# Moving the second group's token rows behind the first modulation's weights, and ordering two helpers behind the first features

## Chip, cores and metric

The kernel runs on one core of one Trainium2 chip. The metric is device time in microseconds: the time of one launch, read as the median of several runs. Lower is better.

## What is computed

One step of a hybrid backbone on 128 context tokens and 1024 latent tokens, width 1024, one layer. The part that matters here is the head of the layer:

```python
def rmsnorm(x, w):
    y = xf * lax.rsqrt(jnp.mean(xf * xf, axis=-1, keepdims=True) + EPS)
    return (y * w.astype(F32)).astype(x.dtype)
...
m = jax.nn.silu(cond) @ w_ada_l + b_ada_l          # six shift/scale/gate vectors of 1024
...
h = rmsnorm(x, norm1_w) * (1 + sc1) + sh1
aq, ak, av, mq, mk, mv, mo, mg = jnp.split(h @ w_in, SPLIT_POINTS, axis=-1)
```

Context tokens take their modulation from `c_ctx`, latent tokens from `c`. After this come grouped-query attention, a bidirectional mLSTM, an output projection and a SwiGLU FFN; none of these is edited.

## The kernel before, in words

The 1152 tokens are nine blocks of 128 (`NB`), taken as three groups of three blocks (`CB`). The tiles x3_0, x3_1 and x3_2 (in views of the profile all called x) hold the rows of the groups. For each group, `normalise(c)` squares the rows on ScalarE with a running sum (L355), takes a reciprocal square root on VectorE by twelve small steps (L127 to L133) and scales the rows on VectorE (L358). `turn(c)` transposes the blocks on TensorE (L116) through PSUM banks and copies one half of each block back on ScalarE (L371) and one on VectorE (L372). `features(c)` applies the modulation: on ScalarE it makes the f16 high part of the features (L507), on VectorE the full value (L508) and the difference (L137), which is the low part. `linear_tok` with `kvg_pairs` then multiplies the features by the key, value and gate columns, three products per piece (L483 to L485), the third of which needs the low part; `evac_kvg` takes the result out on ScalarE (L492, L493) and VectorE (L496, tile G).

The modulation that this needs, shift1 and scale1, is the product of the conditioning with two 1024 x 1024 slices of `w_ada`. They arrive as sixteen loads of 512 KB (L295, tiles aw). TensorE multiplies them in four strips (L341), the strips are copied to SBUF on ScalarE and VectorE (L388, tile part) and turned to columns (L347). From the largest shift and scale follows a power of two (tiles hbd, pv, hsc; L171, L161 to L164, L175, L176) by which both are scaled (L402) before the first feature.

The weights of a projection are held as f16 pairs with a power-of-two scale of their own. `Scaled.ready` loads the raw weights (iraw; kraw for the key, value and gate columns; L193), sums absolute values on ScalarE (L198, tile jkw), reduces them on VectorE (L200) and takes the maximum through TensorE (L116, L171, L161 to L164, L175). `groups_in[0]` are the query weights, the next ones those of the mLSTM heads.

All these loads are issued by SyncE, one behind the other. `ada_rest` loads and multiplies the remaining modulations: eight-row pieces a4 (L422), four buffers, released by the strips on TensorE (L341); at the end of a half it stores a row to g_d (L454) and loads the next bias row (L448).

Each engine runs its instructions in a fixed order that the tile scheduler makes from the order of the code. `tc.high_priority(n)` (`hot`) lets a block go ahead of what was written before it. `tc.issue_after(ins)` keeps what a block issues on the engine of `ins` behind `ins`. `weave` interleaves the units of a generator with those of another.

Of the kernel before, what the change touches and what calls it, by code (L numbers as in the profile page):

```python
# [13 lines left out]
AF = mybir.ActivationFunctionType  # L14
# [7 lines left out]
KD = D // P  # L22
NB = 9
# [10 lines left out]
CB = 3  # L34
# [11 lines left out]
def hybrid_step(ctx: ExitStack, tc: tile.TileContext, I: dict, O: dict):  # L46
# [236 lines left out]

    for b in range(2 * CB):
        load_x(b)
# [6 lines left out]
    for n in range(2):  # L292
        for k in range(KD):
            aw = awp.tile([P, D], F32, name=f"aw0_{n}_{k}")
            dma(aw, w_ada[k * P : (k + 1) * P, n * D : (n + 1) * D])  # L295
            ada_w[n].append(aw)
    for b in range(2 * CB, NB):
        load_x(b)
# [74 lines left out]

    for c in range(2):
        normalise(c)
        turn(c)
    emit(kvg_steps)
# [18 lines left out]
    with hot(300):  # L396
        dve.tensor_reduce(out=hs2, in_=shift1, axis=AX.XY, op=ALU.max, apply_absolute_value=True)
        dve.tensor_reduce(out=hbd, in_=scale1, axis=AX.XY, op=ALU.max, apply_absolute_value=True)
        dve.scalar_tensor_tensor(out=hbd, in0=hbd, scalar=float(D) ** 0.5, in1=hs2, op0=ALU.mult, op1=ALU.add)
        emit(power_scale(gp, one1, hbd, hsc[:, 2:4]))  # L400
        for t in (scale1, shift1):
            dve.tensor_scalar(out=t, in0=t, scalar1=hsc[:, 2:3], scalar2=None, op0=ALU.mult)  # L402
        kvg.inverses()
    es_h = ExitStack()
    kvp = es_h.enter_context(tc.tile_pool(name="kvp", bufs=1, side="right", reuse_waits="tile"))
# [92 lines left out]
    def features(c):  # L498
# [3 lines left out]
        for k in range(KD):  # L502
            full = p0.tile([P, CB, P], F32, name=nm("full"), tag="full", bufs=4)
            for i, n in ((0, 1), (1, 2)) if c == 0 else ((0, CB),):
                cnd = 0 if n == 1 else 1
                s, t = scale1[:, k, cnd : cnd + 1], shift1[:, k, cnd : cnd + 1]
                act(hh[:, k, i : i + n], v[:, k, i : i + n], AF.Identity, scale=s, bias=t)  # L507
                dve.tensor_scalar(out=full[:, i : i + n], in0=v[:, k, i : i + n], scalar1=s, scalar2=t, op0=ALU.mult, op1=ALU.add)  # L508
            sub(hl[:, k], full, hh[:, k], "dve")

    for c in range(NCH):
        with hot(100):
            features(c)
        prods = linear_tok(kvg_pairs, 0, 272, evac_kvg, (tuple(range(c * CB, c * CB + CB)),), bank if c == 1 else bankA)
        if c > 0:
            weave(prods, chain(steps, ada), KD, 10)
        else:
            emit(prods)
        if c == 0:
            normalise(2)  # L520
        if c == 1:
            turn(2)
    emit(steps)
# [1065 lines left out]
```

## Time and profile before

| | |
|---|---|
| three runs | 1562.04, 1564.69, 1565.68 us; median 1564.69 |
| the profiled execution | 1563.28 us, of which the span of the trace is 1561.5 |
| busy, share of the span | PE 95%, PEld 80%, DVE 65%, ACT 49%, POOL 17% |
| mean granted TensorE clock | 0.98 |
| HBM | 183.79 MB read, 13.26 MB written, 126 GB/s over the span |

PE is the matrix product of TensorE, PEld its weight load, DVE VectorE, ACT ScalarE, POOL GpSimd, SP SyncE. A row of the timeline gives start and length in us, engine, line, operation, output and inputs with their shapes, how many instructions are merged, and in brackets the idle time of the engine before it and what ended that. A row of the waits gives who waited for whom: total us, times, longest.

### The profile page before, as it was taken

To read this page: it belongs to the slowest core of one execution; us is meant where nothing else is said; L and a number is where in the kernel's file an instruction comes from. 1 tells how busy PE (TensorE), PEld (TensorE's weight loads), DVE (VectorE), ACT (ScalarE), POOL (GpSimd) and SP (SyncE) were. 2 spreads that over 40 slices of the span, in tenths; PEclk is the share of its full clock that TensorE was granted. 3 is DMA by queue.
4 is the path that set the end of the run, shared out by engine and by line. 5 is a ranking of instruction groups with operands and counts; after the bars stand their busy time and mean duration, and the time that the engine had idled before them with its cause. 6 is when DMAs were issued, how large, how long until landed. Compare 5 with 4: busy or idle time off the path is not lost.

```text
span 1561.5 us, 23390 instructions
## 1 busy us (share of the span) xinstructions
PE 1484.1 (95%) x8539; PEld 1251.8 (80%) x8539; DVE 1017.1 (65%) x2009; ACT 772.3 (49%) x1413; POOL 264.9 (17%) x352
## 2 busy tenths in 40 slices
PE   6799999999988799999999999999999999999997
PEld 3545567677756679899998989989898989999996
DVE  4977555837648674878655577887866584554554
ACT  4854466847644553555432444556552443323333
POOL 0212423322434242000110101000010101001110
PEclk9999999999999799999999999999999999999999
DMA  9664423523356656797654447878763545544441
GB/s 365 201 179 158 85 70 41 120 49 55 79 183 207 201 111 186 192 192 186 151 151 151 142 132 248 185 169 188 176 159 114 169 131 173 162 121 136 148 141 62
DMA packets 387881, 236.91 MB, mean 152 GB/s; under 512 B 170198, under 2 KB 346790, under 8 KB 387766
## 3 DMA queue, kind: packets, MB, share of 16 engines
q1 hardware_dynamic: 384670, 230.26, 54.6%
q10 hardware_dynamic: 3096, 5.16, 1.3%
q8 instruction: 67, 1.10, 0.3%
q14 instruction: 48, 0.39, 0.1%
HBM read 183.79 MB, written 13.26 MB: 126 GB/s over the span
## 4 chain that ended last, share of the span: by engine, by line
PE 58%; DVE 3%; DMA 1%; ACT 1%; issue 0%; POOL 0%; ACTq 0%; DVEq 0%
PE mm L1341 11%; PE mm L1342 11%; PE mm L1340 11%; PE mm L1117 5%; PE mm L1118 5%; PE mm L1119 5%; PE S L1037 3%; PE po L1062 2%; PE po L1061 1%; PE mm L1145 1%; PE mm L1146 1%; PE mm L1147 1%; DVE wlo L137 1%; DMA raw<-in_w_gu_dram 1%; DVE fl L1329 1%; DVE t L1106 1%
## 5 line engine op out<-in xcount | busy, mean ns | idle before, releaser
L152 ACT CAST whi<-raw 128x1024 fp32r<-128x1024 f32 (+1 forms) x216 | 221.7, 1027 | 386.5 <-PE mm L1341 151.0
L137 DVE TENSOR_TENSOR wlo<-raw,whi 128x1024 fp32r<-128x1024 f32 (+1 forms) x216 | 260.1, 1204 | 178.9 <-ACT whi L152 176.3
L1341 PE MATMUL mm<-aTl,whi 128*128 128x384 f32 x1056 | 355.6, 337 | 2.7 <-DVE aTl L137 2.7
L1342 PE MATMUL mm<-aTh,wlo 128*128 128x384 f32 x1056 | 354.3, 336 | 0.0
L1340 PE MATMUL mm<-aTh,whi 128*128 128x384 f32 x1056 | 353.1, 335 | 0.0
L137 POOL TENSOR_TENSOR hl<-tn,hl 128x384 fp32r<-128x384 f32 x66 | 82.5, 1251 | 847.4 <-ACT hl L1363 776.3
L1341 PEld LDWEIGHTS mm<-aTl,whi 128*128 128x128 f32 x1056 | 198.5, 188 | 4.0 <-DVE aTl L137 3.4
L1340 PEld LDWEIGHTS mm<-aTh,whi 128*128 128x128 f32 x1056 | 198.2, 188 | 0.6
L1342 PEld LDWEIGHTS mm<-aTh,wlo 128*128 128x128 f32 x1056 | 198.4, 188 | 0.1
L1118 PE MATMUL mm<-wlo,hl 128*128 128x512 f32 x372 | 145.6, 391 | 0.0
L1117 PE MATMUL mm<-whi,hl 128*128 128x512 f32 x372 | 144.3, 392 | 0.0
L1119 PE MATMUL mm<-whi,hl 128*128 128x512 f32 x372 | 142.9, 392 | 0.0
L483 PE MATMUL wi<-ipair,hT 128*128 128x384 f16 (+2 forms) x408 | 135.0, 334 | 5.2 <-ACT vall L493 2.8
L484 PE MATMUL wi<-ipair,hT 128*128 128x384 f16 (+2 forms) x408 | 135.0, 334 | 0.0
L485 PE MATMUL wi<-ipair,hT 128*128 128x384 f16 (+2 forms) x408 | 131.6, 334 | 1.0 <-DVE hT L137 1.0
L1044 DVE SCALAR_TENSOR_TENSOR pl<-pr,st,ph 128x1152 f16<-128x1152 f32 (+1 forms) x72 | 96.6, 1342 | 34.5 <-ACT ph L1043 33.0
L1039 DVE TENSOR_REDUCE st<-S 128x1 f32<-128x1152 f32 (+1 forms) x72 | 88.9, 1234 | 15.7 <-PE S L1037 14.8
L1040 ACT ACTIVATE pr<-S,st 128x1152 f32<-128x1152 f32 (+1 forms) x72 | 81.4, 1131 | 31.7 <-DVE st L1039 31.0
L1043 ACT ACTIVATE ph<-pr,st 128x1152 f16<-128x1152 f32 (+1 forms) x72 | 83.8, 1163 | 25.5 <-DVE st L1042 12.7
L1037 PE MATMUL S<-kst,qT 128*128 128x384 f32 (+1 forms) x400 | 87.4, 352 | 1.3 <-ACT pr L1040 0.7
L1106 DVE TENSOR_TENSOR t<-mm,gl 128x512 f32<-128x512 f32 x102 | 68.7, 685 | 27.7 <-DMA gl<-g_d 12.2
L1119 PEld LDWEIGHTS mm<-whi,hl 128*128 128x128 f32 x372 | 69.9, 188 | 14.4
(381 smaller groups left out, 2525.3 us busy)
## 6 DMA issues: line engine op xcount, KB each, us to landing
raw<-in_w_gu_dram SPq DMA_DIRECT2D x132, 512.0 KB
raw<-in_w_down_dram SPq DMA_DIRECT2D x60, 512.0 KB
a<-in_w_ada_dram SPq DMA_DIRECT2D x24, 512.0 KB
gl<-g_d SPq DMA_DIRECT2D x36, 256.0 KB
aw<-in_w_ada_dram SPq DMA_DIRECT2D x16, 512.0 KB
iraw<-in_w_in_dram SPq DMA_DIRECT2D x32, 256.0 KB
raw<-in_w_out_dram SPq DMA_DIRECT2D x12, 512.0 KB
x<-in_x_sample_dram SPq DMA_DIRECT2D x11, 512.0 KB
```

The lines of the kernel that those rows point to most:

```text
L137: (dve if eng == "dve" else pool).tensor_tensor(out=out, in0=full, in1=hi, op=ALU.subtract)
L152: nc.scalar.copy(hi[:, :n], raw[:, :n])
L483: mm(ps[:, :n], ah, wh[:, k % 2, c0 : c0 + n], start=(k == 0), stop=False)
L484: mm(ps[:, :n], ah, wl[:, k % 2, c0 : c0 + n], start=False, stop=False)
L485: mm(ps[:, :n], al, wh[:, k % 2, c0 : c0 + n], start=False, stop=(k == KD - 1))
L1037: mm(S[:, n, 0:w], qT[:, h, :], kst[kv][:, t, c0 + n * w : c0 + (n + 1) * w], start=(t == 0), stop=(t == 1))
L1117: mm(ps, ah, wh[:, k % 2, :], start=(k == 0), stop=False)
L1118: mm(ps, ah, wl[:, k % 2, :], start=False, stop=False)
L1119: mm(ps, al, wh[:, k % 2, :], start=False, stop=(k == nk - 1))
L1340: mm(ps, wh[:, k, :], th[:, k, :], start=(k == 0), stop=False)
L1341: mm(ps, wh[:, k, :], tl[:, k, :], start=False, stop=False)
L1342: mm(ps, wl[:, k, :], th[:, k, :], start=False, stop=(k == KD - 1))
```

## The change

Two things are changed. The rows of the second group (x3_1) are loaded after the sixteen modulation weights instead of ahead of the key/value weights, and its `normalise` and `turn` are written behind the modulation. In the loop over the groups, everything that the weaving with the later steps, `normalise(2)` and `turn(2)` issue on ScalarE is kept behind the last ScalarE instruction of the first group's features, which `features` now returns. `tc.issue_after` acts on that engine alone.

```diff
@@ -281,7 +281,7 @@
-    for b in range(2 * CB):
+    for b in range(CB):
         load_x(b)
@@ -294,7 +294,7 @@
             ada_w[n].append(aw)
-    for b in range(2 * CB, NB):
+    for b in range(CB, NB):
         load_x(b)
@@ -371,9 +371,8 @@
-    for c in range(2):
-        normalise(c)
-        turn(c)
+    normalise(0)
+    turn(0)
     emit(kvg_steps)
     kvg_pairs = kvg.pairs(1)
@@ -401,6 +400,8 @@
         kvg.inverses()
+    normalise(1)
+    turn(1)
     es_h = ExitStack()
@@ -504,22 +505,27 @@
-                act(hh[:, k, i : i + n], v[:, k, i : i + n], AF.Identity, scale=s, bias=t)
+                last = act(hh[:, k, i : i + n], v[:, k, i : i + n], AF.Identity, scale=s, bias=t)
...
+        return last.ins
 
     for c in range(NCH):
         with hot(100):
-            features(c)
+            last = features(c)
+            if c == 0:
+                first_last = last
         prods = linear_tok(kvg_pairs, 0, 272, evac_kvg, (tuple(range(c * CB, c * CB + CB)),), bank if c == 1 else bankA)
         if c > 0:
-            weave(prods, chain(steps, ada), KD, 10)
+            with tc.issue_after(first_last):
+                weave(prods, chain(steps, ada), KD, 10)
         else:
             emit(prods)
-        if c == 0:
-            normalise(2)
-        if c == 1:
-            turn(2)
+        with tc.issue_after(first_last):
+            if c == 0:
+                normalise(2)
+            if c == 1:
+                turn(2)
```

What this does to the order on the engines, at three places. In the changed kernel the lines from L388 on move by a few: L387 is the copy of a modulation, L508 and L509 the two halves of a feature, L497 the gates, L673 the reduction of L667.

ScalarE from the copies of the two modulations (part) to the first features, before:

```order
L388 COPY part_383<-wi_365 128x512
L388 COPY part_417<-wi_399 128x512
L355 ACTIVATE jk_620,ssx_619<-x_2_134 128x1024
L355 ACTIVATE jk_622,ssx_619<-x_2_134 128x1024
L355 ACTIVATE jk_624,ssx_619<-x_2_134 128x1024
L198 ACTIVATE jkw,isc_689<-iraw_476 128x512
L507 ACTIVATE hT_439<-x_0_132,shift_88,scale_87 128x128
```

and of the change:

```order
L387 COPY part_321<-wi_303 128x512
L355 ACTIVATE jk_400,ssx_399<-x_1_133 128x1024
L387 COPY part_355<-wi_337 128x512
L355 ACTIVATE jk_402,ssx_399<-x_1_133 128x1024
L355 ACTIVATE jk_404,ssx_399<-x_1_133 128x1024
L371 COPY x_1_133<-mm_425 128x512
L508 ACTIVATE hT_377<-x_0_132,shift_88,scale_87 128x128
```

The squares of the third group (x_2) and the first sum of the query weights have gone from ahead of the features; the squares of the second group (x_1) have come, the first of them ahead of the copy of the second modulation, and one copy of a turned block.

VectorE from the largest modulation (hbd) to the first feature (full), before:

```order
L399 SCALAR_TENSOR_TENSOR hbd<-hbd,hs_116 128x1
L171 TENSOR_REDUCE pv_447<-mm_445 1x1
L161 TENSOR_SCALAR pv_447<-pv_447 1x1
...
L176 COPY hsc<-mm_453 128x2
L129 TENSOR_SCALAR ry_627<-rh_629 128x3
L402 TENSOR_SCALAR scale_87<-scale_87,hsc 128x16
```

and of the change:

```order
L133 SCALAR_TENSOR_TENSOR ry_407<-rt_408,ry_407 128x3
L358 TENSOR_SCALAR x_1_133<-x_1_133,ry_407 128x1024
L176 COPY hsc<-mm_391 128x2
L358 TENSOR_SCALAR x_1_133<-x_1_133,ry_407 128x1024 x2
L401 TENSOR_SCALAR scale_87<-scale_87,hsc 128x16
L401 TENSOR_SCALAR shift_88<-shift_88,hsc 128x16
```

The whole square root of the second group and its three scalings now stand ahead of the scaling of the modulation, and so ahead of the first feature.

VectorE at the scale of the query weights (isc_689, pv_728), before:

```order
L358 TENSOR_SCALAR x_2_134<-x_2_134,ry_627 128x1024 x3
L200 TENSOR_REDUCE isc_689<-isc_689 128x1
L128 TENSOR_SCALAR rh_1118<-rv_1115 128x2
L129 TENSOR_SCALAR ry_1116<-rh_1118 128x2
L131 TENSOR_TENSOR rt_1117<-ry_1116 128x2
L171 TENSOR_REDUCE pv_728<-mm_726 1x1
L132 SCALAR_TENSOR_TENSOR rt_1117<-rt_1117,rv_1115 128x2
L496 SCALAR_TENSOR_TENSOR G<-mm_677,isc_332,gbias 128x2x4
L161 TENSOR_SCALAR pv_728<-pv_728 1x1
```

and of the change:

```order
L358 TENSOR_SCALAR x_2_134<-x_2_134,ry_627 128x1024 x3
L171 TENSOR_REDUCE pv_728<-mm_726 1x1
L132 SCALAR_TENSOR_TENSOR rt_1117<-rt_1117,rv_1115 128x2
L497 SCALAR_TENSOR_TENSOR G<-mm_677,isc_270,gbias 128x2x4 x2
L497 SCALAR_TENSOR_TENSOR G<-mm_678,isc_270,gbias 128x2x4 x2
L497 SCALAR_TENSOR_TENSOR G<-mm_679,isc_270,gbias 128x2x4 x2
L673 TENSOR_REDUCE nrs_1183<-nr_144_1181 128x8
L161 TENSOR_SCALAR pv_728<-pv_728 1x1
```

The reduction L200 now stands five rows ahead of the three scalings of x_2 and no longer behind them; between the maximum (L171) and its next step (L161) stand all six gate steps and the reduction L673.

## The prediction

> **What bounds the kernel now.** I read the stretches first, then the waits, then the rows of the loading stage in order of time.
>
> ```profile
> 0.00:44.60 44.60, 26.90 (x153) 15.79 (x153) 21.84 (x84) 22.72 (x50) 1.21 (x7) 0.91 0.98 366
> 44.60:69.20 24.60, 19.99 (x150) 14.82 (x150) 24.50 (x84) 20.53 (x52) 6.60 (x6) 0.88 0.53 145
> 69.20:94.70 25.50, 20.98 (x181) 12.77 (x181) 20.51 (x58) 16.44 (x29) 4.42 (x5) 1.00 0.81 244
> 94.70:200.00 105.30, 100.72 (x626) 53.53 (x627) 71.06 (x243) 52.28 (x114) 31.68 (x39) 0.98 0.43 119
> ```
>
> The columns are length, busy time of PE, PEld, DVE, ACT and POOL, granted clock, DMA share and GB/s. TensorE is the engine whose gaps set the end: it works 100.72 of the 105.30 us of the last row, while VectorE works 71. The change touches what lies ahead of that row. Three stretches there have different limits. Up to 44.6 us the DMA engines are full (0.98, 366 GB/s). From 44.6 to 69.2 VectorE works 24.50 of 24.60 us while TensorE idles 4.6. From 69.2 to 94.7 nobody is full: it is a chain of waits. Since TensorE is nearly solid after it, a shift of TensorE at about 95 us reaches the end, unless a later gap swallows it. I forecast that shift.
>
> **Step 1, the loads.** SyncE's queue in order of time, and what it waited for:
>
> ```profile
> 26.20 0.33 SPq L295 DMA_DIRECT2D aw<-in_w_ada_dram  x1
> 27.49 0.33 SPq L279 DMA_DIRECT2D x<-in_x_sample_dram  x1
> 34.75 2.93 SPq L193 DMA_DIRECT2D iraw<-in_w_in_dram  x3
> 38.65 0.34 SPq L409 DMA_DIRECT2D kall<-in_cache_k_dram  x1
> ```
> ```profile
> SPq L193 <- DMA aw<-in_w_ada_dram: 3.6, 4, 0.9
> ```
>
> Each issue waits for the landing of a load eight issues earlier, so the issues show the landings: one 512 KB load every 1.29 us (26.20 to 27.49). The fourth `iraw` issue, at about 37.3, marks the sixteenth modulation weight's landing; 38.65 marks that of x_2's first row. Three loads moved behind the weights bring the sixteenth weight to 37.3 - 3 x 1.29 = 33.4. The rows of x_1 land in the freed slots, near 34.7, 36.0 and 37.3; x_2 and all behind it keep their times, since the bytes ahead are the same. Bounds of the head start: two to three slots, 2.6 to 3.9 us; I take 3.9.
>
> **Step 2, where the head start goes.** Rows from the second modulation to the first features:
>
> ```profile
> 32.58 5.81 PE L341 MATMUL wi<-aw,silp 128*32 128x512 f32 x32
> ...
> 38.80 0.58 ACT L388 COPY part<-wi 128x512 f32<-128x512 f32 x1 [9.37 <-PE wi L341]
> ...
> 39.28 1.06 ACT L355 ACTIVATE jk<-x 128x1024 bf16<-128x1024 f32 x1
> 39.44 1.86 PEld L347 LDWEIGHTS wi<-strip_sel,part 128*128 128x128 f32 x16 [1.96 <-ACT part L388]
> ...
> 42.03 0.16 DVE L399 SCALAR_TENSOR_TENSOR hbd<-hbd,hs 128x1 f32<-128x1 f32 x1
> ...
> 44.60 11.91 ACT L507 ACTIVATE hT<-x,shift,scale 128x128 f16<-128x128 f32 x24 [0.91 <-DVE shift L402]
> 44.61 0.34 DVE L508 TENSOR_SCALAR full<-x,scale,shift 128x128 f32<-128x128 f32 x1
> ```
>
> TensorE's block ends at 38.39 and would now end near 34.6. But on ScalarE, as the rows of the order show, the square of x_1's first row now stands ahead of the copy of the second modulation. That row lands at 34.7; with 1.06 us and the accumulator's 0.19 the copy starts at 36.0 instead of 38.80: 2.8 us remain. It does not matter if TensorE's block is up to 1.4 us later than I think, since the square sets this. The other two squares end near 38.9 (37.65 + 1.25). On VectorE the square root's first step, which needs the third square, stands ahead of the last two modulation steps, so `hbd` comes at 39.7 (42.03 - 2.8 = 39.2 without that wait). From `hbd` to the first feature it takes 44.61 - 42.03 = 2.6 now. In the changed order the rest of the square root (about 0.6 us not covered) and x_1's three scalings stand between, and these cost 2.07 by the row of x_2 below. The first feature starts at 39.7 + 2.6 + 0.6 + 2.07 = **45.0**, 0.4 later than now. The head start is spent before the features begin; what it buys is that part of x_1's normalisation is done by then.
>
> **Step 3, the features of groups one and two.** Rows of the stretch in which VectorE is full:
>
> ```profile
> 54.10 0.55 DVE L137 TENSOR_TENSOR hT<-full,hT 128x384 f16<-128x384 f32 x1
> ...
> 55.22 2.24 DVE L137 TENSOR_TENSOR hT<-full,hT 128x384 f16<-128x384 f32 x2
> ...
> 65.03 2.07 DVE L358 TENSOR_SCALAR x<-x,ry 128x1024 f32<-128x1024 f32 x3
> ...
> 67.56 0.27 DVE L171 TENSOR_REDUCE pv<-mm 1x1 f32<-1x128 f32 x1
> ...
> 68.29 0.34 DVE L496 SCALAR_TENSOR_TENSOR G<-mm,isc,gbias 128x8 f32<-128x8 f32 x2
> ...
> 68.69 0.13 DVE L164 TENSOR_SCALAR pv<-pv 1x1 f32<-1x1 f32 x1
> ...
> 69.37 0.68 DVE L667 TENSOR_REDUCE nrs<-nr 128x8 f32<-128x512 f32 x1
> ...
> 72.03 0.69 DVE L372 COPY x<-mm 128x512 f32<-128x512 f32 x1 [0.24 <-PE mm L116]
> ...
> 87.65 0.54 DVE L137 TENSOR_TENSOR hT<-full,hT 128x384 f16<-128x384 f32 x1
> ```
> ```profile
> 62.36 0.63 ACT L198 ACTIVATE jkw<-iraw 128x512 bf16<-128x512 f32 x1
> ...
> 74.68 4.90 ACT L507 ACTIVATE hT<-x,shift,scale 128x384 f16<-128x384 f32 x8
> ```
>
> Added to this full stretch: x_1's three copies, 3 x 0.69 = 2.07 on VectorE, two of the other three on ScalarE, 2 x 0.57 by the copy at 38.80, and x_2's three squares, 3.2, which stood at 39.28 in ScalarE's idle time. ScalarE: 45.0, the sixteen activations of group one (11.91 less group two's eight, 4.90 by the row at 74.68: 7.0), 1.1, 3.2, one weight sum (0.75) and four activations of group two (2.45) put x_2's third square at 59.6. VectorE gets there at about 58.1 (45.0 + 10.0 for what it does now up to the end of the difference at 54.10, + 2.07 + two group-two steps at 0.6, less 0.3 of square root) and stalls 1.5 us, because the square root's first step stands ahead of the differences. The rest took 10.4 up to 65.03; less 1.2 done early, less 1.2 that the pair at 55.22 is slower than two of its kind, plus 0.4: 59.65 + 8.4 = 68.05, **3.0 late**. Bounds: 1.5 (no stall) to 4.2 (the slow pair stays).
>
> **Step 4, the scale of the query weights.** ScalarE's sums end at 63.1 now (62.36 + 0.63 and the accumulator). Behind the features: 62.0 + 0.75 + six evacuations 1.5 + six pieces at 0.75 and one of 0.25 = 69.2. VectorE then reduces (67.02 now), but x_2's scalings (2.07) now stand between this and the maximum (L171), which comes at 72.0 against 67.56. Six `G` steps and the 0.68 us reduction stand between the maximum and the last scale step (L164): that took 1.26, and takes 2.6 with 0.68 and about 0.65 of `G` more. It ends at 74.7 against 68.82: **+5.9**. Bounds: +3 (step 3 alone, if the sums are ready) to +7.
>
> **Step 5, the chain to 94.7.**
>
> ```profile
> 69.18 1.07 PE L341 MATMUL mm<-a,silp 128*32 128x256 f32 x16
> ```
> ```profile
> 80.78 0.36 SPq L454 DMA_DIRECT2D g_d<-row  x1
> 85.59 0.26 SPq L448 DMA_DIRECT2D row<-in_b_ada_dram  x1
> 86.36 1.76 SPq L193 DMA_DIRECT2D iraw<-in_w_in_dram  x3
> ```
> ```profile
> 91.45 0.63 ACT L198 ACTIVATE jkw<-iraw 128x512 bf16<-128x512 f32 x1 [1.47 <-DMA iraw<-in_w_in_dram]
> ...
> 92.95 0.63 ACT L198 ACTIVATE jkw<-iraw 128x512 bf16<-128x512 f32 x1 [0.78 <-DMA iraw<-in_w_in_dram]
> ```
> ```profile
> 94.72 0.52 PE L483 MATMUL wi<-ipair,hT 128*128 128x512 f16 x1 [2.76 <-ACT vall L493]
> ```
>
> The strips of the later modulations stand on TensorE behind the scale; the buffers they free release the next weight loads, behind which SyncE holds the store of g, then the row load that waits for that store, then the head group's weights. All of it moves by about 6: +5.9, and 0.46 of key-cache store that now stands second among those loads, partly hidden: **+6.2** at 86.36. ScalarE then evacuates the third group's projection, behind sums of pieces that it must await. Now three pieces stand ahead (the last starts at 92.95), in the changed order two (91.45): -1.5. TensorE's restart: 94.72 + 6.2 - 1.5 = 99.4. The features of the third group, which must also be done, now end at 88.2 (the row at 87.65), 3.8 before TensorE's stop at 91.97; about 6.3 later that allows 98.3, so they do not decide. TensorE's gap shrinks from 2.76 to 1.1.
>
> **Step 6, the clock.**
>
> ```profile
> 92.00:96.00 4.00, 1.28 (x4) 0.54 (x5) 2.04 (x9) 3.22 (x11) 0.00 (x0) 0.85 0.91 258
> 96.00:100.00 4.00, 4.00 (x15) 1.58 (x14) 3.80 (x10) 2.62 (x8) 0.00 (x0) 0.72 0.22 45
> ```
> ```profile
> 98.35 0.38 PE L483 MATMUL wi<-ipair,hT 128*128 128x512 f16 x1
> 98.56 0.38 PE L484 MATMUL wi<-ipair,hT 128*128 128x512 f16 x1
> ```
>
> After the 2.76 us gap the granted clock fell (0.85, 0.72): nine products took 3.63 us (94.72 to 98.35) where nine at 0.21 take 1.9. With a gap of 1.1 I take no fall: -1.7. Bounds 0 and -1.7. [...]
>
> **Sum.** 6.2 - 1.5 - 1.7 = **+3.0**. The profiled execution took 1563.28 (span 1561.5 and 1.8 around it), 1.4 below the median of the three runs, 1564.69. So 1566.3 for that execution, and 1567.7 as a median. 0.2%, or 3.1 us, is about what a measurement of this kernel can tell from no change.
>
> **Rivals.** *A second fall of the clock.* Between the last group-two product (about 68.9) and the strips (75.1) TensorE has one small transpose in 6 us; the gap at 94.72 shows that 2.76 us can be enough for a fall. The strips, x_2's transposes and the first products would run slower: one stretch like 94.72 to 98.35 costs 1.7, and if the gap at 99 falls too, 1.7 more. Forecast 1569.4 to 1571.1. Against it: VectorE is late there as well and covers most of it. Chance 0.17. [...] *The head start survives* (the other side): the rows of x_1 land with the last weights, so that the squares end before TensorE's block does, at 34.6. Then 38.39 to 44.61 is kept, features start at 40.9, all behind comes 4.1 earlier than worked out: -1.1, 1563.6. It decides at x_1's third landing: before about 34.6 it holds. For it: loads overlap, eight are in flight. Against it: landings are spaced evenly by 1.29. Chance 0.18. *Later gaps swallow it.*
>
> ```profile
> PE wi L809 <- DVE qT L815: 1.7, 1, 1.7
> PE wi L811 <- DVE ipair L219: 1.5, 1, 1.5
> ```
>
> These two gaps lie after 160 us; if their producers do not move with TensorE, 3.0 is taken back: 1564.7. Against it: both follow TensorE's own results. Chance 0.15. My forecast: 0.50.
>
> **Range and chances.** Low end: the head start case less 0.6, 1563.0. High end: both falls of the clock and 0.9 for step 3's upper bound, 1572.0. Slower: 0.30 of my case (the sum lies at the bound, and waits rather add), 0.17, 0.03 = 0.50. Same: 0.20 + 0.07 + 0.10 = 0.37. Faster: 0.11 of the head start case and 0.02 = 0.13.
>
> **What would show it.** Step 1: x_1's first square near 34.7, the second modulation's copy at 36.0. Step 2: first feature at 45.0; at 41 the head start survives. Step 3: last difference of group two near 68, a VectorE wait for ScalarE near 58. Step 4: strips at 75. Step 5: head-group pieces at 97.6. Step 6: no half clock near 100. An early strip (before 72) would break the chain and with it the forecast.

## The result, and the profile after

The changed kernel takes 1569.08 us (median of 9 runs, 1566.3 to 1571.88). The kernel before, run beside it, takes 1563.22 us (9 runs, 1561.04 to 1566.23). The ratio is 1.0033 with a 95% interval of 1.0021 to 1.0045, so the change costs 5.2 us, 3.3 to 7.0 by the interval. The profiled execution of the changed kernel took 1569.08 us (span 1567.3), 5.8 more than that of before. The forecast was +3.0 us, slower by a little: the sign held, the range (1563.0 to 1572.0) holds the result, and 2 to 3 us were missing.

The same four stretches after the change (length, busy time of PE, PEld, DVE, ACT and POOL, granted clock, DMA share, GB/s):

```profile
0.00:44.60 44.60, 24.51 (x135) 13.32 (x136) 18.39 (x74) 17.68 (x40) 1.07 (x7) 0.90 0.96 358
44.60:69.20 24.60, 21.12 (x162) 17.43 (x161) 23.51 (x73) 23.54 (x56) 5.28 (x6) 0.91 0.56 160
69.20:94.70 25.50, 20.38 (x163) 12.77 (x161) 22.21 (x74) 15.49 (x25) 3.28 (x5) 0.87 0.54 171
94.70:200.00 105.30, 99.41 (x624) 52.95 (x623) 71.84 (x238) 51.74 (x113) 30.01 (x34) 0.98 0.50 135
```

The reader is to see three things. The loading stretch moved less (358 GB/s where it was 366). The stretch from 69.2 to 94.7 lost 18 TensorE instructions to later and its clock fell (0.87, was 1.00). And the last stretch, which starts at the same time in both rows, holds 1.3 us less of TensorE's work (99.41 for 100.72): the engine comes to it late and idles more in it.

How far TensorE's instructions of this execution lie behind the same ones of before tells it by place: 5.0 us at the strips (74.14 against 69.18), 5.1 at the restart (99.82 against 94.72), 3.4 nine products later (101.76 against 98.35), 3.0 at 110, 4.7 from 125 on, 5.6 from 175 on. The forecast had 3.0 behind the nine products, close to what came, and assumed that it stays.

**The loads.** First SyncE's issues of the changed kernel, then the stretch from 10 to 15 us of the kernel before and of the changed one:

```profile
2.60 6.96 SPq L193 DMA_DIRECT2D kraw<-in_w_in_dram  x8
...
9.60 14.72 SPq L295 DMA_DIRECT2D aw<-in_w_ada_dram  x16
...
25.27 6.73 SPq L279 DMA_DIRECT2D x<-in_x_sample_dram  x6
```
```profile
10.00:15.00 5.00, 2.62 (x13) 2.62 (x13) 4.56 (x17) 4.23 (x12) 0.00 (x0) 1.00 1.13 320
```
```profile
10.00:15.00 5.00, 0.11 (x2) 0.14 (x4) 3.60 (x13) 3.48 (x14) 0.00 (x0) 1.00 0.94 306
```

The eight small loads of `kraw` (pieces of 256 and 16 columns) now stand directly behind x_0's rows, so that for 7 us (2.60 to 9.56) only they are issued. The first 25 us move about 555 KB less than before (5-us stretches summed). ScalarE's rows show what this does to x_1 (L355), to the copy of the second modulation (L387) and to the first feature (L508):

```profile
36.40 1.06 ACT L355 ACTIVATE jk<-x 128x1024 bf16<-128x1024 f32 x1 [8.23 <-DMA x<-in_x_sample_dram]
37.45 0.56 ACT L387 COPY part<-wi 128x512 f32<-128x512 f32 x1
...
45.09 1.37 ACT L508 ACTIVATE hT<-x,shift,scale 128x128 f16<-128x128 f32 x3
```

x_1's first row comes at 36.40, not at 34.7; ScalarE's copy behind its square at 37.45, not at 36.0; the first feature at 45.09, as forecast.

**The full stretch and the scale.** VectorE's rows of the changed kernel: the square root's wait, the last difference, x_2's scalings, the maximum, the reduction between, and the last scale step:

```profile
59.34 0.32 DVE L127 TENSOR_SCALAR rv<-ssx 128x3 f32<-128x3 f32 x1 [0.98 <-ACT jk L355]
...
68.06 0.54 DVE L137 TENSOR_TENSOR hT<-full,hT 128x384 f16<-128x384 f32 x1
...
69.32 2.08 DVE L358 TENSOR_SCALAR x<-x,ry 128x1024 f32<-128x1024 f32 x3
71.31 0.27 DVE L171 TENSOR_REDUCE pv<-mm 1x1 f32<-1x128 f32 x1
71.58 0.87 DVE L497 SCALAR_TENSOR_TENSOR G<-mm,isc,gbias 128x8 f32<-128x8 f32 x6
72.38 0.66 DVE L673 TENSOR_REDUCE nrs<-nr 128x8 f32<-128x512 f32 x1
...
73.44 0.13 DVE L164 TENSOR_SCALAR pv<-pv 1x1 f32<-1x1 f32 x1
```

TensorE then, and the granted clock (the number behind POOL's) of the two 4-us windows:

```profile
73.63 0.58 PE L175 MATMUL mm<-pv,one 1*128 1x2 f32 x2 [3.92 <-DVE pv L164]
74.14 1.94 PE L341 MATMUL mm<-a,silp 128*32 128x256 f32 x16
```
```profile
72.00:76.00 4.00, 2.37 (x18) 1.09 (x18) 3.84 (x32) 1.56 (x2) 0.87 (x2) 0.60 0.00 0
76.00:80.00 4.00, 4.00 (x22) 2.63 (x22) 1.93 (x11) 1.29 (x3) 2.31 (x2) 0.55 0.86 272
```

A gap of 3.92 us, then a clock of 0.60 and 0.55; the 16 strips take 1.94 us where they took 1.07. That is the rival "second fall of the clock", in its first half.

**The restart.** SyncE's head-group loads, ScalarE's two sums ahead of the evacuation, TensorE's restart, and the clock there:

```profile
93.03 0.95 SPq L193 DMA_DIRECT2D iraw<-in_w_in_dram  x2
```
```profile
97.29 0.63 ACT L198 ACTIVATE jkw<-iraw 128x512 bf16<-128x512 f32 x1 [2.88 <-DMA iraw<-in_w_in_dram]
98.05 0.63 ACT L198 ACTIVATE jkw<-iraw 128x512 bf16<-128x512 f32 x1
```
```profile
99.82 0.38 PE L484 MATMUL wi<-ipair,hT 128*128 128x512 f16 x1 [0.84 <-ACT vall L494]
```
```profile
96.00:100.00 4.00, 3.16 (x18) 1.48 (x16) 0.87 (x5) 2.67 (x10) 0.00 (x0) 1.00 0.91 257
```

Two pieces instead of three, a gap of 0.84, full clock: steps 5 and 6 as forecast, in this execution.

**What came after.** The second pair of the same head group's pieces. Before (SyncE's issue, ScalarE's sum, its square of the keys, its copy of the strips' sum, TensorE's use of it):

```profile
98.30 0.93 SPq L193 DMA_DIRECT2D iraw<-in_w_in_dram  x2
```
```profile
101.08 0.63 ACT L198 ACTIVATE jkw<-iraw 128x512 bf16<-128x512 f32 x1 [2.43 <-DMA iraw<-in_w_in_dram]
...
113.40 1.06 ACT L665 ACTIVATE nr<-qraw 128x1024 f32<-128x1024 f32 x1 [5.72 <-DVE kall L687]
114.36 0.57 ACT L441 COPY part<-mm 128x512 f32<-128x512 f32 x1
```
```profile
115.76 0.95 PE L347 MATMUL mm<-strip_sel,part 128*128 128x2 f32 x8
```

And after:

```profile
103.63 0.93 SPq L193 DMA_DIRECT2D iraw<-in_w_in_dram  x2
```
```profile
106.50 0.63 ACT L198 ACTIVATE jkw<-iraw 128x512 bf16<-128x512 f32 x1 [0.68 <-DMA iraw<-in_w_in_dram]
...
118.51 1.06 ACT L671 ACTIVATE nr<-qraw 128x1024 f32<-128x1024 f32 x1 [6.08 <-DVE kall L693]
119.47 0.57 ACT L442 COPY part<-mm 128x512 f32<-128x512 f32 x1
```
```profile
120.09 1.05 PE L347 MATMUL mm<-strip_sel,part 128*128 128x2 f32 x8 [1.38 <-ACT part L442]
```

Between the sum and the square stands the gates' part: ScalarE's gate steps behind the two sums (the last of them, gd, at 106.21 before and at 110.97 after), then VectorE's scans, and behind them the last step on the keys (kall, at 112.33 and 117.73), for which the square waits. This chain is 5.3 us late at the loads, 5.4 at the sum, 4.8 at gd, 5.4 at kall, 5.1 at the square and the copy, and meets a TensorE that is only 3.0 late. Before, the copy ended 0.8 ahead of its use (114.93 to 115.76); now TensorE waits 1.38 us, and is 4.3 late behind it. What the restart had won was taken back there. Near 162 the changed kernel then has one gap where the kernel before had three, the last of them the 1.7 us quoted with the prediction. Before, and after with its clock:

```profile
161.11 0.34 PE L811 MATMUL wi<-hT,ipair 128*128 128x384 f16 x1 [1.50 <-DVE ipair L219]
...
162.85 0.34 PE L809 MATMUL wi<-hT,ipair 128*128 128x384 f16 x1 [0.43 <-ACT ipair L222]
```
```profile
165.52 0.48 PE L815 MATMUL wi<-hT,ipair 128*128 128x384 f16 x1 [3.57 <-DVE QT L661]
```
```profile
164.00:168.00 4.00, 2.48 (x8) 1.14 (x8) 3.79 (x10) 3.87 (x8) 0.00 (x0) 0.62 0.49 137
```

The waits sum to about the same (1.50 + 0.43 + 1.74 = 3.67 against 3.57), but behind the one long gap the clock fell (0.62), and the shift grows from 4.7 to 5.6, close to the 5.8 of this execution's span.

### The profile page after: what moved, and what is told of

It is laid out like the page before. It is cut to its first block, busy times and chain, and to the rows that moved or that the text cites. A ratio compares the mean times of both kernels' runs of the same rounds, so it can differ in the third digit from the quotient of the medians.

```text
span 1567.3 us, 23380 instructions
## 1 busy us (share of the span) xinstructions
PE 1484.0 (95%) x8539; PEld 1251.8 (80%) x8539; DVE 1017.4 (65%) x2009; ACT 771.9 (49%) x1413; POOL 262.6 (17%) x352
## 5 line engine op out<-in xcount | busy, mean ns | idle before, releaser
L484 PE MATMUL wi<-ipair,hT 128*128 128x384 f16 (+2 forms) x408 | 133.4, 331 | 2.1 <-ACT th L767 1.3
L485 PE MATMUL wi<-ipair,hT 128*128 128x384 f16 (+2 forms) x408 | 133.3, 331 | 0.0
L486 PE MATMUL wi<-ipair,hT 128*128 128x384 f16 (+2 forms) x408 | 129.4, 330 | 0.3 <-DVE hT L137 0.3
L1112 DVE TENSOR_TENSOR t<-mm,gl 128x512 f32<-128x512 f32 x102 | 68.6, 684 | 29.8 <-DMA gl<-g_d 11.2
```

Source lines behind the costliest of these rows:

```text
L484: mm(ps[:, :n], ah, wh[:, k % 2, c0 : c0 + n], start=(k == 0), stop=False)
L485: mm(ps[:, :n], ah, wl[:, k % 2, c0 : c0 + n], start=False, stop=False)
L486: mm(ps[:, :n], al, wh[:, k % 2, c0 : c0 + n], start=False, stop=(k == KD - 1))
```

## The experiments

Each kernel ran beside the kernel before on one chip: runs 1 to 4 on one, 5 to 8 on a second, 9 to 12 on a third. Runs 3 and 12 have 5 executions, the others 11 or 12. "Shift" is how far TensorE's instructions of the profiled execution lie behind the same instructions of before; a single execution of one kernel is good to a few us only, as the sixth run shows. The first column of shifts is that of ScalarE's copy at 114.36, the others TensorE's near that time of before.

| kernel | copy, 114 | 157 | 280 | 700 | 1100 us | ratio, 95% interval |
|---|---|---|---|---|---|---|
| changed | 5.1 | 4.7 | 5.8 | 3.9 | 5.8 | 1.0033, 1.0021 to 1.0045 |
| 6: changed, again | 6.2 | 5.9 | 7.0 | 5.8 | 5.9 | 1.0035, 1.0024 to 1.0045 |
| 1: without the order | 4.5 | 4.3 | 5.8 | 3.0 | 3.0 | 1.0017, 1.0007 to 1.0028 |
| 2: the order alone | 1.9 | 3.0 | 2.9 | 3.7 | 3.7 | 1.0011, 1.0002 to 1.0019 |
| 3: features first | 11.6 | 10.9 | 13.0 | 9.3 | 10.1 | 1.0052, 1.0039 to 1.0065 |
| 4: small loads later | 4.3 | 3.7 | 5.1 | 3.2 | 3.2 | 1.0021, 1.0011 to 1.0030 |
| 5: clock kept | 3.6 | 3.2 | 5.0 | 2.9 | 3.5 | 1.0027, 1.0016 to 1.0039 |
| 7: without x_1's copies | 6.9 | 6.5 | 8.8 | 8.9 | 9.1 | 1.0033, 1.0022 to 1.0045 |
| 8: 1 and 4 together | 0.0 | -0.5 | 1.2 | 0.5 | 0.4 | 1.0029, 1.0015 to 1.0043 |
| 9: scale unbroken | 3.4 | 3.0 | 4.0 | 0.3 | 0.3 | 1.0001, 0.9992 to 1.0010 |
| 10: scale first | -2.8 | 1.4 | 2.1 | -1.3 | -1.3 | 0.9999, 0.9990 to 1.0009 |
| 11: scale first, before | -6.4 | -0.5 | -0.7 | 1.3 | 1.3 | 0.9993, 0.9982 to 1.0003 |
| 12: clock kept, fewer | 5.4 | 5.7 | 7.1 | 6.7 | 7.9 | 1.0053, 1.0039 to 1.0066 |

**1. Without the order.** The changed kernel, its loads and places kept, without `issue_after`.

```diff
-            with tc.issue_after(first_last):
-                weave(prods, chain(steps, ada), KD, 10)
+            weave(prods, chain(steps, ada), KD, 10)
...
-        with tc.issue_after(first_last):
-            if c == 0:
-                normalise(2)
-            if c == 1:
-                turn(2)
+        if c == 0:
+            normalise(2)
+        if c == 1:
+            turn(2)
```

> The loads moved and the second group's normalisation behind the modulation, as in the changed kernel, but nothing ordered behind the first features: x_2's squares and the first two sums of the query weights go back ahead of them on ScalarE. Theory A (the order pushes the scale of the query weights late, and strips, head-group loads and TensorE's restart follow it): VectorE loses the stall at 59, the strips come at 69.5 to 71 instead of 73.9, the head group's loads at 88 instead of 93.0, TensorE's restart at 96 instead of 99.8; ratio to the kernel before 1.0005 to 1.0018, about 1564.8 where before is 1563.2. What is left then is x_2's rows landing 1.5 late, so features up to 1 us later. Theory B (the loads cost it: the DMA engines move less in the first 20 us and all behind lands 1.5 us late, so the shift is there with or without the order): strips stay within 1 us of 73.9, ratio 1.003 to 1.004.

Measured: 1.0017; strips at 72.58, 1.6 earlier than with the order. ScalarE's first feature comes at 46.73, since a sum of a weight piece stands ahead of it, while VectorE's comes at 45.30. Restart after a gap of 3.0, with the clock down again (0.57 from 100 to 104). So the loads and places alone cost about half of the change by the middle values; the interval overlaps with that of the whole.

**2. The order alone.** The kernel before, loads and places as they were, with the two `issue_after` and `first_last` of the change.

```diff
+        return last.ins
...
-            features(c)
+            last = features(c)
+            if c == 0:
+                first_last = last
...
+            with tc.issue_after(first_last):
+                weave(prods, chain(steps, ada), KD, 10)
...
+        with tc.issue_after(first_last):
```

> The kernel before with only the third group's norm, the sums of the query weights and the rest of that weaving ordered behind the first features; loads and the second group's normalisation stay where they were. Theory A: first features at 44.6 as before, but x_2's squares and all eight query-weight sums behind them on ScalarE, and on VectorE the query weights' reduction now stands behind four of the six gate steps: strips at 72 to 75, restart of TensorE at 98 to 101; ratio 1.002 to 1.004. Theory B (the loads cost it): ratio within 0.999 to 1.001.

Measured: 1.0011; features at 45.05, strips at 71.59 (before 69.18), the clock at 0.50 from 72 to 76, head-group loads at 89.84. The order alone delays the scale: x_2's squares now stand in the full stretch (56.86 to 61.7, before from 39.28), and the reduction L200 comes at 69.05 instead of 67.02. The two parts, 1.0017 and 1.0011, make the 1.0033 to 1.0035 of the whole within their intervals; neither part is what the cost hangs on alone.

**3. Features first.** x_1's normalisation and turn behind the first group's features.

```diff
-    normalise(1)
-    turn(1)
     es_h = ExitStack()
...
             if c == 0:
                 first_last = last
+        if c == 0:
+            with tc.issue_after(first_last):
+                normalise(1)
+                turn(1)
```

> The changed kernel with the normalisation and turning of x_1 put behind the first group's features on ScalarE, so that the head start of the weights reaches the features. The second modulation's copy no longer waits for a square. First feature at 40.5 to 41.5 instead of 45.1. x_1's squares then follow the sixteen activations (48.6 to 52). Theory A: VectorE's full stretch starts 3.5 us earlier but stalls about 1 us for x_1's squares, the strips come at 70.5 to 72 instead of 73.9, about 2.5 us less than the changed kernel: ratio 1.001 to 1.002. Theory B' (the features' start is what counts, and all 3.5 us are kept): strips at 70, ratio 1.000 to 1.001. If x_1's normalisation in the full stretch costs what the earlier start brings, ratio 1.003.

Measured: 1.0052, a miss twice over. The first feature comes at 43.48, 1.6 earlier and not 4, and what was moved away is late afterwards: x_1's squares start at 50.50, its scaling at 59.88, TensorE waits 5.3 us for it, strips at 80.73. The head start that step 2 saw spent is not worth having at the price of x_1.

**4. The small loads later.** The key, value and gate weights' loads behind the first eight modulation weights.

```diff
     kvg_steps = kvg.ready()
-    next(kvg_steps)
...
             ada_w[n].append(aw)
+        if n == 0:
+            next(kvg_steps)
```

> The changed kernel with the eight loads of the key, value and gate weights moved behind the first modulation's eight weights, so that 512 KB weight loads follow x_0 directly. It asks whether these smaller loads are what lowers the throughput of the first 20 us (327 and 306 GB/s in two stretches of 5 us, where the kernel before has 410 and 320) and so makes x_1's first row land at 36.4 instead of the forecast 34.7. If so: the first modulation's weights land earlier, all bytes behind them too, x_1's first row at 34.7 to 35.2, first feature at 43.5 to 44; under theory A the chain behind takes 1 of it: ratio 1.002 to 1.003; under theory B all 1.5: ratio 1.002. If the throughput loss has another cause (three x rows alone in flight at the start), the row lands at 36.4 again and the time stays at 1.003.

Its stretch from 10 to 15 us:

```profile
10.00:15.00 5.00, 5.00 (x18) 1.14 (x18) 4.24 (x18) 0.00 (x0) 0.39 (x1) 1.00 1.00 388
```

Measured: 388 GB/s where the changed kernel moved 306, and the shortfall by 25 us is 330 KB instead of 555. The slow stretch went along with the small loads: from 20 to 25 us run 4 moved 349 GB/s, where the kernels before and after moved 414 and 417. The first features come 0.8 earlier (44.26), the strips no earlier (74.60). Where x_1's first row lands cannot be read: its square (37.10) now stands behind the copy of the second modulation, which waited for TensorE until 36.62. The clock stays at 1.00 from 72 to 84. The ratio is 1.0021; it overlaps with 1.0035, so the gain of about 2 us is likely and not shown. That less was moved where the small loads stood is shown for these stretches (306 against 388, 349 against 417 GB/s); that this is the whole of step 1's miss is not, as 60% of the shortfall stays.

**5. The clock kept.** 22 products whose sums nobody reads stand between the transposition and the broadcast of the scale, to fill the gap of 3.92 us.

```diff
         ps = bank()
+        for _ in range(fill):
+            mm(ps[:, 8:392], hTh[0][:, 0, 0:128], hTh[0][:, 0, 0:384], start=True, stop=True)
         mm(ps[:, 0:2], one, v[:, 2:4], start=True, stop=True)
```

> The changed kernel with 22 products (128x384, their sums are not used) put on TensorE between the transposition of the query weights' maximum at 69.4 and the product that waits for the scale (73.6), so that TensorE does not idle 3.9 us there. It prices the fall of the clock alone. Theory A: with the clock kept at full, the first sixteen strips take 1.07 instead of 1.94 and x_2's transposes end 2 to 3 us earlier (at 79.5 to 80.5 instead of 82.3); third group's features, head group's loads and TensorE's restart follow by 1.5 to 3: ratio to the kernel before 1.0015 to 1.0025. Rival C: what is slow after 74 is waited for anyway (the loads of the strips' weights land when they land), so TensorE waits longer for them and the end does not move: ratio 1.003 to 1.004.

```profile
71.49 3.73 PE L176 MATMUL mm<-hT 128*128 128x384 f16 x22 [1.93 <-DVE pv L171]
75.16 1.06 PE L343 MATMUL mm<-a,silp 128*32 128x256 f32 x14
```

Measured: 1.0027. The clock stays at 1.00 from 72 to 84, the strips take 1.06 again, and x_2's transposes end at 81.0 instead of 82.3. But the products could not start before 71.49 (they waited for VectorE's maximum, L171), and ran to 75.2, 1.7 past the scale. The gain by the clock and the loss by the overrun cannot be told apart in 1.0027.

**6. The changed kernel once more,** without an edit, on the chip of runs 5, 7 and 8.

> The changed kernel once more, as it stands, on the same chip as the other three. It tells what part of the 1.0033 belongs to one chip or one profile, and whether the step of 1.9 us between 973 and 1002 us, which stands in the first profile of the changed kernel and in none of the four experiments so far, comes again. If that step is chance: a shift of 3.5 to 4.5 us against the kernel before at 1100 us, ratio 1.0020 to 1.0030. If it belongs to the kernel: 5.5 to 6 us, ratio 1.003 to 1.004.

SyncE's head-group loads and TensorE's restart:

```profile
94.08 1.10 SPq L193 DMA_DIRECT2D iraw<-in_w_in_dram  x2
```
```profile
101.00 0.38 PE L484 MATMUL wi<-ipair,hT 128*128 128x512 f16 x1 [2.62 <-DVE G L497]
```

Measured: 1.0035, as at first, but this execution comes to its loss in another way. The head-group loads are 7.7 late (6.7 at first), the restart 6.3 late, so the 1.4 of the two pieces came again. But behind the gap of 2.62 the clock fell (0.71 and 0.86 from 100 to 108), as in the kernel before, so the 1.7 of step 6 did not come. TensorE does not wait for the copy (L347 starts at 121.42, 0.27 behind the copy's end), and the shift stays near 6. In the first execution the 1.7 came and was taken back 15 us later. By either way it does not reach the end. The clock fell behind the scale here too (0.80 and 0.78 from 72 to 80, behind a gap of 3.16). The step of 1.9 between 973 and 1002 us does not come again (5.9 at both), and the ratio is the same without it: that step belongs to one execution, the level does not.

**7. Without x_1's copies.** VectorE's three copies of x_1's turned rows (2.07 us) are left out, so that the second half of x_1's columns stays unturned in the computation.

```diff
-    turn(1)
+    turn(1, True)
...
-            dve.tensor_copy(x[:, 512:1024], pss[1])
+            if not half_only:
+                dve.tensor_copy(x[:, 512:1024], pss[1])
```

> The changed kernel without VectorE's three copies of x_1's turned blocks (3 x 0.69 us): the second half of x_1's turned rows stays unturned, so that work is left out. In the kernel before these copies stood in VectorE's idle time ahead of 38 us; the change puts them into the stretch from 45 to 69 us in which VectorE is full. Theory A: group two's last difference comes 2 to 3 us earlier (65.5 to 66.5), the strips at 71 to 72.5, and the end follows by 1.5 to 2.5: ratio 1.0015 to 1.0025. Rival B (the late landing of the loads sets the shift): strips within 1 us of 73.9, ratio 1.003.

```profile
70.06 0.27 DVE L171 TENSOR_REDUCE pv<-mm 1x1 f32<-1x128 f32 x1
70.46 2.06 DVE L358 TENSOR_SCALAR x<-x,ry 128x1024 f32<-128x1024 f32 x3
...
73.11 0.66 DVE L674 TENSOR_REDUCE nrs<-nr 128x8 f32<-128x512 f32 x1
...
74.02 0.13 DVE L164 TENSOR_SCALAR pv<-pv 1x1 f32<-1x1 f32 x1
```

Measured: 1.0033, nothing gained. The last difference starts at 67.12 (68.06 in the changed kernel) and not at 65.5 to 66.5. The maximum comes 1.25 earlier (70.06), and the time to the last scale step grows from 2.1 to 4.0, as x_2's scalings and the reduction now stand in it. My theory that the scale is late by the work added to VectorE fell here in its simple form: what is taken away is filled up by other ready work. What decides is which instructions stand *inside* the chain from maximum to scale. This led to runs 9 to 11.

**8. Runs 1 and 4 together.**

> Both single steps that helped, together: key, value and gate weights loaded behind the first modulation's weights (1.0021 alone) and nothing ordered behind the first features (1.0017 alone). If the two gains against the changed kernel add up (1.9 and 2.5 us of 5.2): ratio 1.0004 to 1.0008, about the kernel before. If both shorten the same wait: 1.0015. Theory A says the former, with the strips at 71 to 72.5 and no fall of the clock between 72 and 80.

Measured: 1.0029. The gains of runs 1 and 4 did not add up, and single executions spread from 1563.74 to 1574.9. The profiled one was the shortest of them (features at 40.95, all shifts near 0) and does not stand for the median. Inconclusive.

**9. The scale unbroken.** The changed kernel; the gate steps of group two and the keys' reduction (L673) are ordered behind the last scale step.

```diff
-        powers(v, 1)
+        last_power.append(powers(v, 1).ins)
...
+        with tc.issue_after(last_power[-1]) if b // CB == 1 else ExitStack():
             for t in range(2):
...
+            with tc.issue_after(query_power):
                 norm_rope(qp, cc, ss, kall[:, b : b + 4], 4, NKV, kw, (b, b + 4))
```

> The changed kernel with VectorE's gate steps of group two and the reduction L673 (with the rope that follows it) ordered behind the last step of the query weights' scale (L164), so that nothing long stands between the maximum (L171) and L164. In the changed kernel that took 2.1 us and once 2.4, where the kernel before takes 1.1. Theory A: L164 starts at 72.1 to 72.5 instead of 73.4, the strips at 72.4 to 72.8, TensorE's gap is 2.8 instead of 3.9; third group and head group's loads 1 to 2.5 earlier; ratio 1.0018 to 1.0028. If the end does not hang on this chain: 1.003 to 1.004.

```profile
72.58 0.27 DVE L173 TENSOR_REDUCE pv<-mm 1x1 f32<-1x128 f32 x1
...
73.30 0.13 DVE L164 TENSOR_SCALAR pv<-pv 1x1 f32<-1x1 f32 x1
73.36 0.87 DVE L500 SCALAR_TENSOR_TENSOR G<-mm,isc,gbias 128x8 f32<-128x8 f32 x6
```

Measured: 1.0001, an interval apart from that of run 6. From maximum to scale step 0.72 us instead of 2.13; from the first feature to the scale step 26.7 instead of 28.3 (the features of this execution started 1.5 later, which hides the gain in the clock time of the strips, 73.96). The clock fell behind the scale here too (0.77 and 0.81 from 72 to 80, behind a gap of 2.52). Of the 5.3 us that it wins (0.0034 of 1564), 2 to 3 are there at 157 us; the rest arises between 280 and 700, where its shift falls from 4.0 to 0.3. Of this, 2.1 come between 440 and 470, where the clock of the kernel before falls twice (at 453.22 and 463.46, for 3.41 us each) and that of run 9 once (mean clock 0.96 and 0.98 from 400 to 480); by half of 3.41 one fall is worth 1.7 us (an estimate). In the same stretch 796 TensorE instructions stand at another place in the order than in the changed kernel; but so do 811 in run 3 and 658 in run 12, which are slower. The first part goes with the shorter scale chain; what the second follows from is not settled.

**10. The scale first.** Run 9, and x_2's scalings behind the scale step too.

```diff
             if c == 0:
-                normalise(2)
+                scale_x2 = normalise(2)
             if c == 1:
+                with tc.issue_after(last_power[-1]):
+                    scale_x2()
                 turn(2)
```

> As the run before, and x_2's three scalings (2.08 us) also ordered behind the query weights' scale. Then VectorE reduces and scales as soon as ScalarE's sums end (68.3): L171 at 69.3, L164 at 70.0, strips at 70.4, no gap long enough for a fall of the clock; x_2's turned blocks start about 1.5 us later on VectorE than they could but 3 us earlier than in the changed kernel (its first transposes at 76.0). Theory A: third group's features 3 earlier, head group's loads at 90 instead of 93, ratio 1.0008 to 1.0020. If what bounds is the work of VectorE up to the third group's features (the same in both), ratio 1.003.

```profile
72.27 0.28 DVE L173 TENSOR_REDUCE pv<-mm 1x1 f32<-1x128 f32 x1 [1.75 <-PE mm L116]
```

Measured: 0.9999. Strips at 73.66, not 70.4: VectorE was free 1.75 us earlier, and the maximum waited for TensorE, which had the rest of group two's products ahead of the transposition. TensorE came to them late: the features of this execution start 1.2 later (46.28), and the clock was at 0.75 from 64 to 68. Its gap at the scale shrank to 0.96, and the clock stayed at 1.00 (72 to 76 us).

**11. The same edits in the kernel before.**

> The same rearrangement of VectorE in the kernel before: query weights' scale ahead of x_2's scalings, gate steps and the reduction behind it. There the sums end at 63.1 and the reduction L200 waited behind the scalings (67.02); now L200 at 65.0, L171 at 66, L164 at 66.8, strips at 67.1 instead of 69.2; x_2's transposes at 68.5 to 69.5 instead of 70.2. Theory A: head group's loads and TensorE's restart come 1 to 2 us earlier, and the kernel is faster than the kernel before: ratio 0.9985 to 0.9995. If the loads of the strips' weights or the gate chain on ScalarE bound it: ratio 1.000.

Measured: 0.9993, not to be told from no change. Strips at 68.29, shift -3.0 at 140 us, and 2.5 of it gone by 146, where TensorE waits 1.04 us (until 141.64) and its 16 strips take 1.93 us (1.07 at 69.18 in the kernel before, at a clock of 1.00); the rest goes between 280 and 700 us (from -0.7 to 1.3). On this chip the changed kernel with the scale first (0.9999) and the kernel before with it (0.9993) overlap: ordered so, the change costs nothing that can be measured.

**12. The clock kept with fewer products.** Run 5 with 10 of them.

> The run with products in TensorE's gap again, with 10 instead of 22 of them: the 22 started at 71.5, when their bank came free, and ended at 75.2, 1.7 us after the scale was there. Ten end at 73.2, about when the scale comes, so that the strips start at 73.6 to 73.9 as in the changed kernel, but at full clock: x_2's transposes end at 79.0 to 79.6 instead of 82.3 (81.0 with 22 products). Theory A (the fall costs what it delays x_2's turn by, of which half reaches the end): ratio 1.0013 to 1.0025. Rival C (the end does not hang on it): 1.003 to 1.0035. The two parts of the gap, 1.9 us and at most 0.5, should bring no fall.

```profile
99.17 0.59 PE L487 MATMUL wi<-ipair,hT 128*128 128x512 f16 x1 [2.60 <-DVE G L500]
```

Measured: 1.0053, far above what the clock theory allowed. The clock was kept from 68 to 84, as meant, and x_2's transposes ended at 79.3, as expected. But the edit sorted ScalarE's work anew: three pieces stand ahead of the evacuation again (the third at 96.35), TensorE's gap is 2.60 long and the clock falls there instead. A kernel with the clock kept at the scale is thus no faster for it: the second fall of the clock happened, but taking it away alone does not bring the time back.

## Why the prediction was right in sign and short in size

1. **The loads.** The mechanism was right, the size off: x_1's row came at 36.40, not 34.7. The step gave every load the same slot of 1.29 us wherever it stands; in run 4, with the small loads later, the stretch from 10 to 15 us moves 388 GB/s for 306, and 225 of the 555 KB come back by 25 us.
2. **The head start.** Spent, as forecast (45.09 against 45.0), but by two misses that cancel: `hbd` came at 40.68 instead of 39.7, and from it to the first feature it took 4.4 instead of 5.3.
3. **The full stretch.** Right, and a little short: a stall of 0.98 (forecast 1.5); the last difference starts at 68.06 and ends at 68.6, 3.5 later than before, where the forecast had its end at 68.05, 3.0 later.
4. **The scale.** +4.75 (the last step ends at 73.57, before at 68.82) against +5.9: the sums were ready earlier (68.3; forecast 69.2, where its own terms add up to 69.0), so the maximum came at 71.31 for 72.0, and from its start to the end of the last step it took 2.26 us for 2.6. From start to start these are 2.13, and run 9 shows that this can be cut to 0.72.
5. **Loads and restart.** +6.7 for +6.2, near by luck: two misses cancel, since the strips were 5.0 late for 5.9 and between them and the loads 1.7 came in for 0.3. Two pieces instead of three, the restart at 99.82 for 99.4, the gap 0.84 for 1.1. In run 6 the loads are 7.7 late, and two pieces again.
6. **The clock at the restart.** In the first execution nine products took 1.94 us, as forecast; in run 6 the clock fell again. That a gap of 1.1 would bring no fall was my choice between the two bounds: the gap of 0.84 brought none (1.00 from 96 to 104), the one of 2.62 in run 6 did (0.71 from 100 to 104).

**The step that failed** is the last term of the sum, the -1.7 of step 6, with what stood under it: that a shift of TensorE at about 95 us reaches the end, unless a later gap swallows it. I looked for gaps that give time back and not for chains that take it. The head group's last two pieces left SyncE 5.3 us late and were still 5.1 late in ScalarE's copy, whose slack had been 0.8; so TensorE could not be less than 5.1 - 0.8 = 4.3 late behind L347, whatever it won at its restart, and 4.3 is what it was. Where the clock fell again (run 6), the 1.7 never came. Without that term the sum is 4.7 by the forecast's own numbers (6.2 - 1.5), 5.1 by the first execution's (6.7 less 1.6), 6.3 by run 6's; the runs have 5.2 and 5.5 (0.0033 and 0.0035 of 1563). The loads' 0.5 to 1.5 more than forecast and the fall of the clock at 165 us (0.9) are the smaller misses.

**The rivals.** The head start did not survive. The later gaps at 160 us swallowed nothing: their sum stayed, 3.6 to 3.7 us. Between 280 and 550 us one execution gave back 4 (5.8 to 1.8) and lost as much later, the other only 0.6 (7.0 to 6.4); the medians show nothing of it. The second fall of the clock happened (0.60 and 0.55 from 72 to 80), in run 6 too (0.80, 0.78). Its forecast of 1569.4 to 1571.1 lies 0.3 us above the result. What the fall does close by can be read: from the strips to the head-group loads the shift grew by 1.7, 2.5, 1.9, 1.1 and 2.7 us in five executions in which the clock fell at the strips (the changed kernel, runs 6, 1, 2 and 7; 0.60, 0.80, 0.60, 0.50 and 0.50 from 72 to 76) and by 0.1 to 0.5 in three more (runs 8, 9 and 11; 0.86 from 68 to 72, 0.77 from 72 to 76 and 0.66 from 68 to 72); in four without this fall (runs 4, 5, 10 and 12; 1.00 from 72 to 80) it changed by -0.7, -0.9, -1.3 and 0.5. But the end does not follow: runs 4 and 5, without that fall, still are at 1.0021 and 1.0027, run 12 at 1.0053, and run 9, with it, at 1.0001. It is not the cause of the size alone.

What stays open: how much of run 9's gain is the shorter scale chain, and how much arose later with the other order and the clock near 460 us; what the fall at 74 us costs at the end; and how the loss is split, since the two executions of one kernel split it differently.

## What to carry to other kernels

A delay that a chain of loads carries can reach an engine in more than one place (here TensorE at its restart, 5.1 us late, and again behind ScalarE's copy, 4.3): follow every instruction that the late loads release, with its slack, before subtracting a gain at the first place where they meet. On a full engine under a scheduler, work that is taken away can be refilled with whatever is ready (run 7: 2.07 us of copies left out, the last scale step at 74.02 for 73.44); if a short chain must end early, order the rest behind it, and read what stands inside the chain rather than how much stands ahead of it. And one execution of a kernel tells a mechanism, while a cost of 2 or 3 us in 1565 needs the runs: the same kernel reached the same time by two different ways.

## What the hardware showed that was not expected

- **Gaps of one length were followed by half clock in one execution and by full clock in another.** The kernel before has a gap of 2.34 us up to 462.46, the changed kernel one of 2.34 us up to 466.72. Behind the first the granted clock was 0.50 from 463.46 to 466.87 (the first two rows: the stretch that ends where the fall begins, and the fall); behind the second it stayed at 1.00 (the last two rows: the stretch with the end of the gap, and the next):

```profile
460.05:463.46 3.41, 1.07 (x10) 0.98 (x10) 3.41 (x11) 1.20 (x5) 1.47 (x2) 1.00 0.00 0
463.46:466.87 3.41, 3.41 (x24) 1.78 (x23) 2.15 (x14) 0.37 (x2) 1.15 (x1) 0.50 0.15 29
```
```profile
465.33:468.74 3.41, 2.02 (x26) 1.58 (x26) 3.41 (x15) 0.63 (x2) 0.46 (x2) 1.00 0.01 2
468.74:472.15 3.41, 3.41 (x27) 2.76 (x20) 2.85 (x11) 1.43 (x5) 2.11 (x1) 1.00 0.67 209
```

  In the same way a gap of 2.18 us (up to 59.29) and one of 0.78 behind it were followed by a fall in run 12 (0.88 from 64 to 68), while gaps of 2.17 (up to 59.96) and 0.96 in the changed kernel were not (1.00 from 56 to 68). What decides it is not shown by these rows.
- **The stretch with the small loads moved less.** Behind eight loads of 256- and 16-column pieces the stretch from 10 to 15 us moved 306 GB/s; with 512 KB loads in the same stretch, 388. In run 4, with the small loads later, the slow stretch is later too (349 from 20 to 25 us, where the changed kernel has 417).
- **Ordering small groups of VectorE's instructions moved the order of hundreds of others,** up to 580 us into the kernel (run 9: 871 of TensorE's 8,539 instructions stand elsewhere). This is the scheduler's doing and not the chip's, and what it is worth is not shown.
